# A hybrid decoder layer on one core: engine orders fixed by a table, wider value products, the solve's row spread in two fp32r passes

## The chip, the core and the metric

The kernel runs on one core of a Trainium2 chip. Five engines work from queues of their own, each strictly in the order of its queue: TensorE (PE, with its weight loads PEld), VectorE (DVE), ScalarE (ACT), GpSimd (POOL) and SyncE (SP), which issues most DMAs here. They meet at semaphores. The metric is the device time of one execution in microseconds, the median of several runs; lower is better.

## The reference

One decoder layer over 512 tokens of width 1024, batch 1, all in float32. Two mixers share an input projection: sparse attention with 8 heads in 2 groups, and a gated DeltaNet with 4 heads of width 128 in chunks of 64. Cut to what matters:

```python
def reference(x, w_in, ...):
    h = x @ w_in[l]
    y_a = nsa_attention(nsa_q, cmp_k, cmp_v, slc_k, slc_v, win_k, win_v, nsa_gate, ...) @ w_nsa_out[l]
    y_b = gated_deltanet(gdn_qkv, gdn_beta, gdn_decay, gdn_gate, ...) @ w_gdn_out[l]
    mix = (sigmoid(gate_a) * y_a + sigmoid(gate_b) * y_b) @ w_o[l]
    x = layer_norm(DEEPNORM_ALPHA * x + mix, ln1_g[l], ln1_b[l])
    f = conv_ffn(x, ffn_w_up[l], ffn_conv_w[l], ffn_w_down[l])
    return layer_norm(DEEPNORM_ALPHA * x + f, ln2_g[l], ln2_b[l])

def nsa_attention(...):
    o = g[0] * o_cmp + g[1] * o_slc + g[2] * o_win     # three softmax branches, each probabilities @ values

def gated_deltanet(...):
    qkv = silu(causal_dwconv(qkv, conv_w))             # four taps per channel
    m = where(strict, einsum('bhncd,bhnsd->bhncs', kb, k) * decay, 0.0)
    T = lax.linalg.triangular_solve(eye + m, eye, left_side=True, lower=True, unit_diagonal=True)
    # u = T @ (v*beta), w = T @ (kb*exp(gcum)), then a scan over the chunks
```

With 8 blocks of 64 keys and the best 8 chosen, the selected branch sees all causal keys, as the window branch of 512 does.

## The kernel before

**Precision.** Most products are made of three fp32r products: each operand is split into a rounded part (wh, xh, mh) and a remainder (wl, xl, ml), and `product` adds rounded x rounded, rounded x remainder and remainder x rounded in PSUM (L262, L264, L265). ACT rounds a weight block (L248; or DVE or POOL, L250), DVE or POOL forms its remainder (L252). Small products of the mixers run in plain fp32.

**Stages.** `token_major` projects what is needed with tokens on the partitions (PSUM tiles pb) while x arrives. Then come 40 projections of 128 columns each (`gemm_t`, PSUM tile gps in two banks, 24 products of 512 columns for one). They are the work with which PE fills the time of the two mixers. After the mixers come the output projections (pm), the projection w_o with the first normalisation (pw), the FFN's up-projection (pu, 22 steps of two), and its down-projection (px, py, pz) by a scheme with sums of weight blocks, which POOL forms by eight adding DMAs (`sums`, wsum).

**DeltaNet, for each of the 4 heads.** `gdn_k`, `gdn_q` and `gdn_v` make a projection, a convolution of four taps and SiLU: the first tap goes from PSUM into acc on ACT (L405), three more follow on DVE (L413) or, by a table, as an ACT product and a POOL sum (L410, L411). The projection's PSUM bank is free again when the last tap has read it. `gdn_mid` makes decays and the matrix m from products of k with k and q (L507). `gdn_tri` starts the triangular solve with blocks of 16 rows: lo is the masked m, f16 its sums folded to 16 columns, gx spreads f16 over rows with the mask "row", and a product with the block mask "same" sums over partitions (L529; first 512, then 256 columns). Fifteen dependent pairs of small DVE instructions (tmp L536, xs L537) invert the blocks, and z (L539) puts them back on the diagonal. `gdn_inv` joins blocks of 16 to 32, 64 and 128 (transposes of z, products of z with m and ym with x), `gdn_out` runs over the four pieces of 128 tokens, `gdn_gate` ends it.

**Attention, for each of the 8 heads.** Units of query blocks t (128 tokens) and branches: `scores` makes scores (L806, L807), exponentials and the scaling; `flip` transposes the probabilities sc (L839) into slots of pth (rounded) and ptl (remainder) and multiplies by the values vcat into pout (L856). The order of units was (branch 0, t 2), (0, 3), (1, 2), (1, 3), (both, 0), (both, 1). Of a product, 256 columns are two query blocks, t 0 and 1 or t 2 and 3, for one key block; a zeroed slot stands where key block 3 meets t 2.

**What sets the order.** ORDER is a list of steps (q queries, k keys, p and c compression, a and b the halves of a head's attention, i j v m n w o y the DeltaNet steps named above, g a merge gate), each recorded with a priority; SHIFT moves a step's priority, ENGINE says which of DVE, ACT and POOL does a given instruction. A scheduler puts the instructions in order by these priorities and by its own view of when each is ready.

Of the kernel before, what the change touches and what calls it, by code (L numbers as in the profile page):

```python
# [130 lines left out]
BUFS = {"w2": 2, 'in': 3, 'st': 6, 'mid': 3, 'out': 5, 'att': 3, 'ob': 1, 'qf': 2, 'kq': 2, 'lx': 1, 'pg': 2, 'pd': 2, 'pa': 3, 'raw': 3, 'wh': 3, 'wl': 3, 'q2': 4, 'mg': 6, 'mr': 3}


@with_exitstack
def body(ctx: ExitStack, tc: tile.TileContext, d, out):
# [205 lines left out]
    upper_r = nsa.tile([128, 128], F32R, name="upper_r")  # L341
    gcw = tiny[:, 0:48].rearrange("p (i h j) -> p i h j", i=3, h=4)
# [171 lines left out]
    def gdn_tri(h):  # L514
# [5 lines left out]
        f16 = sp.tile([128, TT, 16], F32, name="f16", bufs=2)  # L520
        V.tensor_reduce(f16, lo.rearrange("p c (b j) -> p c j b", b=8), axis=AX.X, op=OP.add)
        lx = slot("lx", "lx", (128, TT, 16, 16))
        for r0, n in ((8, 16), (0, 8)):
            rs = slice(r0, r0 + 8)
            sh = (128, TT, 8, n)
            gx = slot("mid", "gx", sh)
            E(f"gx{n}", h).tensor_tensor(gx, bc(f16[:, :, None, :n], sh), bc(C["row"][:, None, rs, None], sh), op=OP.mult)
            pl = dps(sh)
            PE.matmul(pl, C["same"], gx, start=True, stop=True)  # L529
            A.activation(lx[:, :, rs, :n], pl, AF.Copy)  # L530
# [258 lines left out]
    for t in (pth, ptl):  # L789
        G.memset(t[:, :, 6, :].bitcast(F32), 0.0)  # L790
# [35 lines left out]
    def flip(h, u, s):  # L826
# [18 lines left out]
        if t % 2 == 0:  # L845
            return
# [10 lines left out]
        if u < 5:  # L857
            return
# [407 lines left out]
```

## Time and profile before

| what | us |
|---|---|
| median of 3 runs | 851.35 |
| lowest and highest of them | 846.26, 852.24 |
| the profiled execution | 847.99 |
| its span, first to last instruction | 846.2 |
| PE busy in the span | 826.3 |

The profile is of one execution. The span is what all its views divide. "Busy" of PE runs from a product's start to the end of its drain, so that short pauses between products do not show as idle; the chain of work that ended last gives instead the piece of time for which each instruction held the end back. A group's row has line, engine, operation, out<-in, shapes and count, then busy us and mean ns of one, then idle before and who ended it. A row of the waits says which instruction waited for which: us in total, how often, the longest. In rows of instructions in time, the first two columns are the start and the length; x4 means four records together, and a product in plain fp32 leaves two records. In windows each row is a stretch, with the busy time of each engine, its instructions in brackets, the granted share of PE's clock, and the DMA's share and GB/s.

### The profile page before, as it was taken

The page shows a single profiled execution, that of the slowest core. Times are in us where ns is not written, and L with a number is a line of the kernel's source. Part 1 is how long each engine was busy: PE and PEld are TensorE (multiplying, and loading weights), DVE is VectorE, ACT ScalarE, POOL GpSimd, SP SyncE. Part 2 cuts the span into 40 slices and gives each one's busy share as a digit, 9 for nine tenths or more (in the row PEclk, how much of TensorE's full clock was granted, in tenths as well). Part 3 has the DMA queues.
Part 4 walks back from the last instruction along what each step waited for, and adds up shares of the span by engine and source line. Part 5 has one row for each costly group of instructions (what it writes and reads, how often), then busy time and mean ns, then how long its engine had stood idle before and what let it go on. Part 6 is the DMA issues. An engine that isn't in the chain of part 4 may idle for free.

```text
span 846.2 us, 11884 instructions
## 1 busy us (share of the span) xinstructions
PE 826.3 (98%) x4226; PEld 681.4 (81%) x4226; DVE 597.3 (71%) x1276; ACT 403.0 (48%) x890; POOL 164.3 (19%) x160
## 2 busy tenths in 40 slices
PE   9899899999999999999999999999999999999996
PEld 8777688777778778888888898888888888887874
DVE  5855579986867866674457637777777777768786
ACT  4464377575456777532234113444444444556531
POOL 0354442233136111102200003111112111100000
PEclk9999899999999999999999999999999999999998
DMA  7223111002101110254346007998975922575662
GB/s 273 95 83 100 54 48 51 26 26 75 45 32 66 35 51 26 88 178 134 125 137 237 25 2 269 266 244 253 205 223 153 225 88 77 161 247 176 198 213 100
DMA packets 35051, 108.05 MB, mean 128 GB/s; under 512 B 3248, under 2 KB 4400, under 8 KB 34608
## 3 DMA queue, kind: packets, MB, share of 16 engines
q1 hardware_dynamic: 27696, 84.23, 30.6%
q0 software_dynamic: 7296, 23.07, 11.5%
q8 instruction: 33, 0.54, 0.3%
q14 instruction: 26, 0.21, 0.1%
HBM read 105.19 MB, written 25.17 MB: 154 GB/s over the span
## 4 chain that ended last, share of the span: by engine, by line
PE 84%; DVE 10%; DMA 2%; issue 2%; ACT 1%; SPq 0%; POOL 0%; DVEq 0%; ACTq 0%; POOLq 0%
PE pu L262 9%; PE pu L264 9%; PE pu L265 9%; PE gps L262 7%; PE gps L264 7%; PE gps L265 7%; PE px L1147 5%; PE pz L1147 3%; PE pout L856 2%; PE aps L839 2%; PE pw L1022 2%; PE pw L1023 2%; PE pw L1021 2%; PE pm L265 2%; PE pm L262 2%; PE pm L264 2%
## 5 line engine op out<-in xcount | busy, mean ns | idle before, releaser
L252 DVE TENSOR_TENSOR wl<-raw,wh 128x512 fp32r<-128x512 f32 x140 | 114.1, 816 | 66.9 <-ACT wh L248 62.5
L248 ACT ACTIVATE wh<-raw 128x512 fp32r<-128x512 f32 x136 | 85.5, 631 | 151.4 <-PE pu L264 103.8
L262 PE MATMUL pu<-mh,wh 128*128 128x512 f32 (+1 forms) x384 | 142.7, 372 | 0.0
L264 PE MATMUL pu<-ml,wh 128*128 128x512 f32 (+1 forms) x384 | 142.6, 371 | 0.0
L265 PE MATMUL pu<-mh,wl 128*128 128x512 f32 (+1 forms) x384 | 142.6, 371 | 0.0
L262 PE MATMUL gps<-xh,wh 128*128 128x512 f32 x320 | 129.3, 405 | 3.6 <-DVE xs L537 2.2
L264 PE MATMUL gps<-xl,wh 128*128 128x512 f32 x320 | 129.1, 404 | 0.0
L265 PE MATMUL gps<-xh,wl 128*128 128x512 f32 x320 | 126.8, 398 | 0.0
L265 PEld LDWEIGHTS pu<-mh,wl 128*128 128x128 f32 x384 | 72.3, 188 | 12.6
L262 PEld LDWEIGHTS pu<-mh,wh 128*128 128x128 f32 x384 | 72.3, 188 | 12.4
L264 PEld LDWEIGHTS pu<-ml,wh 128*128 128x128 f32 x384 | 72.3, 188 | 12.4
L262 PEld LDWEIGHTS gps<-xh,wh 128*128 128x128 f32 x320 | 60.4, 189 | 16.6 <-issue 2.9
L1103 DVE SCALAR_TENSOR_TENSOR fa<-pu,fcw,fa 128x511 f32<-128x511 f32 x88 | 65.7, 746 | 10.7 <-ACT fa L1100 9.2
L265 PEld LDWEIGHTS gps<-xh,wl 128*128 128x128 f32 x320 | 60.6, 189 | 10.8 <-issue 0.2
L264 PEld LDWEIGHTS gps<-xl,wh 128*128 128x128 f32 x320 | 60.6, 189 | 10.2 <-issue 0.2
L1109 POOL TENSOR_TENSOR fth<-fth,fa 128x512 f32<-128x512 f32 x22 | 28.6, 1302 | 201.8 <-DVE fa L1103 201.8
L252 POOL TENSOR_TENSOR wl<-raw,wh 128x512 fp32r<-128x512 f32 x36 | 46.3, 1288 | 83.0 <-ACT wh L248 68.8
L1080 ACT ACTIVATE wh<-raw 128x512 fp32r<-128x512 f32 x67 | 40.5, 627 | 39.8 <-DMA raw<-wsum 11.1
L1081 DVE TENSOR_TENSOR wl<-raw,wh 128x512 fp32r<-128x512 f32 x67 | 43.8, 685 | 19.4 <-ACT wh L1080 19.2
L812 ACT ACTIVATE sc<-sc,mn 128x384 f32<-128x384 f32 (+2 forms) x64 | 35.8, 560 | 12.9 <-DVE mn L810 10.7
L295 POOL TENSOR_TENSOR rs<-rs,minus_half 128x1 f32<-128x1 f32 x8 | 7.6, 945 | 166.5 <-DVE rs L980 166.5
L1100 ACT ACTIVATE fa<-pu,fcw 128x512 f32<-128x512 f32 x44 | 29.6, 672 | 10.2 <-PE pu L265 10.2
(330 smaller groups left out, 1689.5 us busy)
## 6 DMA issues: line engine op xcount, KB each, us to landing
raw<-in_up SPq DMA_DIRECT2D x44, 512.0 KB, 4.8
raw<-in_wT SPq DMA_DIRECT2D x40, 512.0 KB, 3.5
wsum<-in_down POOLq DMA_DIRECT2D x6, 2816.0 KB, 24.5
raw<-wsum SPq DMA_DIRECT2D x20, 512.0 KB, 4.2
raw<-in_down SPq DMA_DIRECT2D x15, 512.0 KB, 4.4
wsum<-wsum POOLq DMA_DIRECT2D x2, 2816.0 KB, 12.3
raw<-in_wm SPq DMA_DIRECT2D x8, 512.0 KB, 3.6
raw<-in_wo SPq DMA_DIRECT2D x8, 512.0 KB, 3.6
```

What stands on the lines that cost most here:

```text
L248: A.activation(wh, r, AF.Copy)
L252: eng.tensor_tensor(wl, r, wh.bitcast(F32), op=OP.subtract)
L262: i = PE.matmul(ps, wh[k], mh_(k), start=(k == 0), stop=False)
L264: PE.matmul(ps, wh[k], ml_(k), start=False, stop=False)
L265: PE.matmul(ps, wl[k], mh_(k), start=False, stop=(k == n - 1))
L812: A.activation(s[:, i, :n], s[:, i, :n], AF.Exp, scale=-1.0, bias=mn[:, 0, i:i + 1], accum_out=mn[:, 1, i:i + 1])
L1080: A.activation(hi, raw[:, i], AF.Copy)
L1081: V.tensor_tensor(lo, raw[:, i], hi.bitcast(F32), op=OP.subtract)
L1100: A.activation(acc, ps, AF.Copy, scale=w[:, 2:3])
L1103: V.scalar_tensor_tensor(acc[:, n:], ps[:, :S - n], w[:, i:i + 1], acc[:, n:], op0=OP.mult, op1=OP.add)
L1109: G.tensor_tensor(th, th, g[1], op=OP.mult)
L1147: m = PE.matmul(ps, a[x][:, j, ts], w[y], start=first and i == 0, stop=last and i == 2, skip_group_check=True)
```

## The change

**The order.** SHIFT, ENGINE and ORDER have new entries. A new table QUEUES lists for each engine its instructions by number, the number being the place at which the kernel's code makes the instruction. After the body, `queues` ties every instruction to the one ahead of it in the table by an edge that sets the order only and waits for nothing at run time. So the scheduler's choice is replaced by the table, instruction by instruction. In all, the runs of numbers cover 3904 products of PE (3960 before).

**The value products.** The units now go (both, 0), (both, 1), (0, 2), (0, 3), (1, 2), (1, 3). pth and ptl have 13 slots per branch in place of 8; key block k and query block t stand at slot 3k + t. The products of a branch come together after its t 3: key block 0 against all four query blocks (512 columns), 1 against three (384), 2 and 3 against two (256; the zeroed slot is 11).

**The row spread.** f16 gets three parts: the sum, its rounded part and the remainder. Two gx tiles in fp32r are made and multiplied by a rounded copy same_r of the mask, adding up in PSUM. [...]

**Room.** The scratch of the DMAs that POOL issues is set to 4096 bytes per partition.

```diff
+QUEUES = {
+    "PE": """0-9 11-12 10 13-48 50 53 56 49 51-52 54 62-63 59 57 60 64 61 55 71 65 58 66 74-76 68 67 77 72 78 69-70 73 79 89 80 83
...
+def queues(tc):
+    made = {k: [] for k in QUEUES}
+    for i in tc.nc.cur_bb.bb.instructions:
+        k = str(i.engine).split(".")[-1]
+        if k in made and type(i).__name__ != "BassTilePoolBoundary":
+            made[k].append(i)
+    for k, runs in QUEUES.items():
+        last = None
+        for run in runs.split():
+            a, _, b = run.partition("-")
+            for n in range(int(a), int(b or a) + 1):
+                i = made[k][n]
+                if last is not None:
+                    tc.add_manual_dep(i, last.name, mybir.DependencyInfo(
+                        mybir.DependencyClass.NoSync, mybir.DependencyReason.SCHED_ONLY), reason="place in its queue")
+                last = i
...
+        G.tensor_copy(same_r, C["same"])
...
-        f16 = sp.tile([128, TT, 16], F32, name="f16", bufs=2)
-        V.tensor_reduce(f16, lo.rearrange("p c (b j) -> p c j b", b=8), axis=AX.X, op=OP.add)
+        f16 = sp.tile([128, 3, TT, 16], F32, name="f16", bufs=2)
+        V.tensor_reduce(f16[:, 2], lo.rearrange("p c (b j) -> p c j b", b=8), axis=AX.X, op=OP.add)
+        V.tensor_copy(f16[:, 0].bitcast(F32R), f16[:, 2])
+        V.tensor_tensor(f16[:, 1], f16[:, 2], f16[:, 0], op=OP.subtract)
...
-            gx = slot("mid", "gx", sh)
-            E(f"gx{n}", h).tensor_tensor(gx, bc(f16[:, :, None, :n], sh), bc(C["row"][:, None, rs, None], sh), op=OP.mult)
             pl = dps(sh)
-            PE.matmul(pl, C["same"], gx, start=True, stop=True)
+            for i, e in enumerate(("gx", "gy")):
+                gx = slot("mid", "gx", sh, F32R)
+                E(f"{e}{n}", h).tensor_tensor(gx, bc(f16[:, i, :, None, :n], sh), bc(C["row"][:, None, rs, None], sh),
+                                              op=OP.mult)
+                PE.matmul(pl, same_r, gx, start=(i == 0), stop=(i == 1))
...
-    UNITS = [((0, 2),), ((0, 3),), ((1, 2),), ((1, 3),), ((0, 0), (1, 0)), ((0, 1), (1, 1))]
+    UNITS = [((0, 0), (1, 0)), ((0, 1), (1, 1)), ((0, 2),), ((0, 3),), ((1, 2),), ((1, 3),)]
...
-        for br, _ in parts:
-            for k in range(4 if t > 1 else 2):
-                o = pout[:, 256:] if t > 1 else pout[:, :256]
-                b = 2 * k if t > 1 else 4 + 2 * k
-                w = vcat[:, k, br, g].rearrange("p a b -> p (a b)")
-                for i, src in enumerate((pth, ptl)):
-                    PE.matmul(o, w, src[:, br, b:b + 2, :], start=(u == 1 and k == 0 and i == 0), stop=False)
-        if u < 5:
+        for k in range(4):
+            c = min(k, 2)
+            w = vcat[:, k, br, g].rearrange("p a b -> p (a b)")
+            for i, src in enumerate((pth, ptl)):
+                PE.matmul(pout[:, 128 * c:], w, src[:, br, 3 * k + c:3 * k + 4, :],
+                          start=(br == 0 and k == 0 and i == 0), stop=False)
+        if br == 0:
             return
...
+        queues(tc)
```

**Where rows moved.** DVE at the end of the first head's solve, before: tmp and xs are the solve's steps (the last number of the shape is what is left of the block), acc the convolution taps of a projection gps.

```order
L536 TENSOR_TENSOR tmp<-lx,xs 128x4x3
L537 TENSOR_TENSOR xs<-xs,tmp 128x4x3
L536 TENSOR_TENSOR tmp<-lx,xs 128x4x2
L413 SCALAR_TENSOR_TENSOR acc<-gps,tiny,acc 128x511
L537 TENSOR_TENSOR xs<-xs,tmp 128x4x2
L413 SCALAR_TENSOR_TENSOR acc<-gps,tiny,acc 128x510
L536 TENSOR_TENSOR tmp<-lx,xs 128x4
L413 SCALAR_TENSOR_TENSOR acc<-gps,tiny,acc 128x509
L537 TENSOR_TENSOR xs<-xs,tmp 128x4
L539 TENSOR_TENSOR z<-xs,cst 128x512
```

The same solve on DVE now, some steps after its start (kq is the end of another projection's SiLU):

```order
L681 TENSOR_TENSOR tmp<-lx,xs 128x4x13
L554 SCALAR_TENSOR_TENSOR acc<-gps,tiny,acc 128x510
L554 SCALAR_TENSOR_TENSOR acc<-gps,tiny,acc 128x509
L682 TENSOR_TENSOR xs<-xs,tmp 128x4x13
L681 TENSOR_TENSOR tmp<-lx,xs 128x4x12
L682 TENSOR_TENSOR xs<-xs,tmp 128x4x12
L564 SCALAR_TENSOR_TENSOR kq<-th,acc 128x4x128
L681 TENSOR_TENSOR tmp<-lx,xs 128x4x11
L554 SCALAR_TENSOR_TENSOR acc<-gps,tiny,acc 128x511
L682 TENSOR_TENSOR xs<-xs,tmp 128x4x11
L681 TENSOR_TENSOR tmp<-lx,xs 128x4x10
L554 SCALAR_TENSOR_TENSOR acc<-gps,tiny,acc 128x510
```

The taps that stood among the last three of the fifteen step pairs stand among the third to the sixth; one more stands just ahead of the solve and one behind its last step, and z of this head is in POOL's queue.

PE at the first head's spread products, before (aps rows belong to the compressed branch):

```order
L265 MATMUL gps<-xh,wl 128x512
L529 MATMUL dps<-gx,cst 128x512
L741 MATMUL aps<-cu,w_692 128x62
L529 MATMUL dps<-gx,cst 128x256
L747 MATMUL aps<-w_692,gv 128x64 x2
L262 MATMUL gps<-xh,wh 128x512
L264 MATMUL gps<-xl,wh 128x512
```

And now, from the eleventh projection product behind the first spread product (of the rounded part, 512 columns) on:

```order
L403 MATMUL gps<-xl,wh 128x512
L886 MATMUL aps<-cu,w_663 128x62
L892 MATMUL aps<-w_663,gv 128x64 x2
L404 MATMUL gps<-xh,wl 128x512
L674 MATMUL dps<-gx,same_r 128x256
L674 MATMUL dps<-gx,same_r 128x512
```

Two products side by side have become four, spread over 17 projection products, and 61 instead of 49 projection products follow before the first transpose of z.

SP near the start, before:

```order
L214 DMA xr_128<-in_xT 128x512
L218 DMA wB_133<-in_wB 128x576
L214 DMA xr_129<-in_xT 128x512
L241 DMA raw<-in_wT 128x1024 x3
L337 DMA tiny<-in_tiny 128x57
L338 DMA cst<-in_consts 128x1444
L339 DMA ident<-in_consts 128x128
```

And now (xr are slices of x, raw the weight blocks, cst the masks, fcw the FFN's taps; ident went earlier still, ahead of the last five slices of x):

```order
L353 DMA xr_128<-in_xT 128x512
L491 DMA fcw<-in_fcw 128x132
L357 DMA wB_133<-in_wB 128x576
L850 DMA pos<-in_pos 128x32
L353 DMA xr_129<-in_xT 128x512
L476 DMA tiny<-in_tiny 128x57
L380 DMA raw<-in_wT 128x1024
L477 DMA cst<-in_consts 128x1444
L380 DMA raw<-in_wT 128x1024 x6
```

The small constants moved ahead of the last slice of x, and the masks ahead of the second weight block.

More of the change, by code (lines that the diff above doesn't have):

```diff
@@ new lines @@
+1405 1330 1230 1293-1294 1406 1408 1407 1409 1295-1296 1410-1413 1231-1232 1297 1422-1423 1298-1299 1414 1300
+1415-1418 1424-1426 1419-1420 1427 1379-1380 1428 1381-1383 1421 1384-1387 1429-1432 1443-1444 1388 1331-1332
+1389-1391 1433 1392 1434-1435 1445-1446 1436-1438 1447 1439-1440 1448 1441 1449 1453-1454 1393 1442 1301 1394 1450
+1333 1395-1398 1455 1458 1451-1452 1456-1457 1459 1399 1302-1303 1400 1304-1306 1460-1463 1401 1472-1473 1334 1464
+1402 1474-1480 1501 1465 1481-1482 1502 1466-1468 1483 1469-1470 1503 1335 1504 1336-1338 1471 1339-1342 1505-1506
@@ new lines @@
+3874-3875 3845-3858 3876-3879 3859 3880-3881 3860-3865 3882 3866-3870 3883-3903""",
+    "DVE": """0 27 104 1-4 6 5 7 9 8 10-11 13 12 14-15 17 16 18-19 58-61 64 28 22 20 65 23 66 62 67 25 21 63 90 115 72 31-35 73
+36-37 24 38-42 30 43 29 44 26 45-50 102 51-52 74 53-54 68-69 83 55-56 70-71 81 84 82 92-93 85-87 94 75 88 80 76 79 95
+151-153 77 91 107 154 109 164 110-111 108 112 89 113 96-100 166 101 103 165 114 167 212 155 116-118 285 119 105 120
+156-157 121-123 158 124 168 125-126 169 127-128 57 129 106 130-133 78 134-136 170 137-138 213 139-145 172 146-147 173
@@ new lines @@
+55 48 42 51 49 62 47 52 92 66 37 67-68 64 69 57 65 46 58 50 87 56 53 59 61 63 88 90 60 80 75 77 76 86 78 84 71 85
+72-73 70 94 81 74 82 93 91 89 95 79 96-97 83 98-130 132 131 133-134 136 135 137 139 138 140 142 141 143 145 144
+146-147 149 148 150 152 151 153-163""",
+    "SP": """0-7 17 8-12 18 13 25 14-15 19 16 20-23 26-31 24 32-78 84-86 79-81 87-90 82 91 83 92-128 130-135 129 136-159 161 163
+165 167-168 160 162 169 164 166 170-178""",
+}
+def queues(tc):
[14 more added lines that the diff above has]
+                last = i
@@ L341, in body @@
     upper_r = nsa.tile([128, 128], F32R, name="upper_r")
+    same_r = nsa.tile([128, 128], F32R, name="same_r")
     gcw = tiny[:, 0:48].rearrange("p (i h j) -> p i h j", i=3, h=4)
@@ L785, in cmp_attn @@
         PC[g] = (hi, lo)
-    pth = nsa.tile([128, 2, 8, 128], F32R, name="pth")
-    ptl = nsa.tile([128, 2, 8, 128], F32R, name="ptl")
+    pth = nsa.tile([128, 2, 13, 128], F32R, name="pth")
+    ptl = nsa.tile([128, 2, 13, 128], F32R, name="ptl")
     for t in (pth, ptl):
-        G.memset(t[:, :, 6, :].bitcast(F32), 0.0)
-    UNITS = [((0, 2),), ((0, 3),), ((1, 2),), ((1, 3),), ((0, 0), (1, 0)), ((0, 1), (1, 1))]
+        G.memset(t[:, :, 11, :].bitcast(F32), 0.0)
+    UNITS = [((0, 0), (1, 0)), ((0, 1), (1, 1)), ((0, 2),), ((0, 3),), ((1, 2),), ((1, 3),)]
     POUT = {}
@@ L839, in flip @@
                 PE.transpose(pt[:, i, k, :], s[:, i, k * 128:(k + 1) * 128], ident)
-        first = t - 2 if t > 1 else 4 + t
-        own = (slice(br, br + len(parts)), slice(first, first + 2 * t + 1, 2))
+        own = (slice(br, br + len(parts)), slice(t, 4 * t + 1, 3))
         th, tl = pth[:, own[0], own[1], :], ptl[:, own[0], own[1], :]
```

108 lines of the change are left out of this document (102 added, 6 removed), and 5 rows, old and new, of the table QUEUES.

## The prediction

> **What bounds the kernel now.** I read the page first: the engine totals, the granted clock in 40 slices, the chain of work that ended last.
>
> ```profile
> PE 826.3 (98%) x4226; PEld 681.4 (81%) x4226; DVE 597.3 (71%) x1276; ACT 403.0 (48%) x890; POOL 164.3 (19%) x160
> PEclk9999899999999999999999999999999999999998
> PE 84%; DVE 10%; DMA 2%; issue 2%; ACT 1%; SPq 0%; POOL 0%; DVEq 0%; ACTq 0%; POOLq 0%
> ```
>
> PE is busy for 826.3 of 846.2 us, so a change pays where it shortens PE's own work or one of PE's few waits. DVE has 10% of the chain: the waits are mostly for it. The windows say where PE is not full (after the length come PE, PEld, DVE, ACT and POOL busy, then the granted clock).
>
> ```profile
> 0.00:350.00 350.00, 339.81 (x1982) 276.63 (x1983) 251.94 (x757) 204.15 (x568) 106.42 (x108) 0.99 0.21 67
> 350.00:846.00 496.00, 486.54 (x2246) 404.79 (x2244) 345.33 (x519) 198.85 (x323) 57.90 (x52) 0.99 0.58 170
> ```
>
> Up to 350 us, the mixers, PE lacks 350 − 339.8 = 10.2 us. From there on the order of PE's products is unchanged but for the interleaving of the first merges; that stage's 9.5 us (the tail of the down projection and the last normalisation) I leave as they are. PE's own waits by name:
>
> ```profile
> PE gps L262 <- DVE xs L537: 2.2, 1, 2.2
> PE gps L327 <- DVE vm L324: 1.4, 1, 1.4
> PE gps L262 <- ACT tap L410: 1.2, 1, 1.2
> PE dps L395 <- issue: 1.1, 1, 1.1
> PE px L1147 <- ACT w L1080: 0.9, 1, 0.9
> PE aps L839 <- DVE xs L537: 0.6, 1, 0.6
> PE pz L1147 <- DVE wl L1081: 0.6, 1, 0.6
> PE dps L427 <- DVE z L558: 0.5, 1, 0.5
> ...
> PE dps L427 <- POOL z L539: 0.5, 1, 0.5
> PE dps L529 <- DVE gx L527: 0.5, 1, 0.5
> ```
>
> Without the start (L327) and the tail (L1147), the six rows for the mixers besides the first make 4.4 us. The largest wait, in order of time (start, length, engine and line):
>
> ```profile
> 88.24 1.32 POOL L252 TENSOR_TENSOR wl<-raw,wh 128x512 fp32r<-128x512 f32 x1 [0.30 <-ACT wh L248]
> ...
> 88.45 1.14 DVE L537 TENSOR_TENSOR xs<-xs,tmp 128x16 f32<-128x16 f32 x1
> ...
> 89.84 0.17 DVE L537 TENSOR_TENSOR xs<-xs,tmp 128x12 f32<-128x12 f32 x1
> ...
> 91.69 0.75 DVE L413 SCALAR_TENSOR_TENSOR acc<-gps,tiny,acc 128x509 f32<-128x509 f32 x1
> ...
> 92.59 0.65 PE L262 MATMUL gps<-xh,wh 128*128 128x512 f32 x1 [2.21 <-DVE xs L537]
> ```
>
> The projection wants its PSUM bank, which is free once DVE has read it in the convolution taps (acc, L413). These stand in DVE's queue behind the steps of the solve, so the wait put down to xs is really for the taps. A solve step of 0.17 us takes 1.14 us where it starts under a POOL product. And the clock falls right behind the wait:
>
> ```profile
> 88.00:92.70 4.70, 2.49 (x12) 1.79 (x10) 4.48 (x13) 0.33 (x2) 1.32 (x1) 1.00 0.36 112
> 92.70:99.50 6.80, 6.74 (x26) 5.86 (x27) 2.08 (x5) 2.73 (x5) 3.18 (x3) 0.50 0.00 1
> ```
>
> 6.8 us at 0.50 cost 3.4 us. The episode is worth 2.2 + 3.4 = 5.6 us.
>
> **The change, part by part.** What a product costs PE is its distance to the next start, not its duration, in which the drain is counted. The chain gives the distances.
>
> ```profile
> 125.68 0.83 PE pout L856 x7
> ...
> 131.95 0.17 PE aps L807
> ...
> 142.23 0.44 PE aps L839 x4
> ...
> 144.28 0.11 PE aps L839
> 144.39 0.24 PE gps L264
> ```
> ```profile
> 730.28 14.29 PE px L1147 x63
> ```
>
> So 256 columns cost 0.83/7 = 0.119 us, 384 columns 0.17 us (the L807 row here is the one of that width), 512 columns 14.29/63 = 0.227 us.
>
> *Value products.* Per head, branch and part (rounded, remainder) six products of 256 columns, 0.711 us, become one of 512, one of 384 and two of 256: 0.227 + 0.17 + 0.237 = 0.637 us. There are 8 x 2 x 2 = 32 such groups: −2.4 us. PE is full beside them, so all of it counts. Ends: 0, if the products wait for later transposes instead (they now start only when all four row blocks of a branch are there), and −4.0, if the 8 groups less also save a change of precision of 0.2 us each (below). I take −2.4; it is plain counting on a full engine.
>
> *Row spread.* One fp32 product of 512 and one of 256 columns now, and the projection behind them:
>
> ```profile
> 215.11 1.53 PE L529 MATMUL dps<-gx,cst 128*128 128x512 f32 x4 [0.47 <-DVE gx L527]
> ...
> 216.29 0.58 PE L262 MATMUL gps<-xh,wh 128*128 128x512 f32 x1
> ```
>
> Start to start 1.18 us; the four fp32r products are 2 x (0.227 + 0.119) = 0.69 us. Four heads: 4 x 0.49 = −2.0 us. Ends: −3.4 us by the 1.53, and 0, if the longer chain ahead of the product takes it back. That chain gains a rounding and a subtraction of 128x64 and a second gx of each width:
>
> ```profile
> L521 DVE TENSOR_REDUCE f<-lo 128x64 f32<-128x512 f32 x4 | 4.2, 1057 | 1.2 <-POOL lo L519 1.1
> ...
> L527 DVE TENSOR_TENSOR gx<-f,cst 128x512 f32<-128x512 f32 x4 | 3.2, 807 | 0.0
> ...
> L537 DVE TENSOR_TENSOR xs<-xs,tmp 128x60 f32<-128x60 f32 x4 | 1.0, 238 | 0.0
> ...
> L527 DVE TENSOR_TENSOR gx<-f,cst 128x256 f32<-128x256 f32 x2 | 0.8, 411 | 0.0
> ```
>
> With 0.24 for each of the first two (nearest row, 60 columns), that is up to 0.48 + 0.81 + 0.41 = 1.7 us a head, 6.8 us of DVE and POOL in a stage where DVE is idle for 350 − 251.9 = 98 us. It lies beside other work of PE where there is enough between the products of k and the first gx product. In the first head that cover shrinks from 42 projection products and 16 others to 7 and the 16 of the compression, each of which leaves two records:
>
> ```profile
> 68.16 2.37 PE aps L721 x16
> ```
>
> 2.37/8 = 0.30 us each, so 7 x 0.227 + 16 x 0.30 = 6.3 us, against a chain of lo and the wide gx on POOL (1.32 each by the wl row above), the reduction 1.06, the rounding 0.24 and half a microsecond for m, 4.4 us. Behind the gx pair on POOL there wait a root of the norms and three weight remainders. The third head, where PE waits for gx today (0.5), has 13 projections and 8 others for 6 and 20, about as much cover, and 0.24 us more to cover. I add 0.5 us; without any cover it would be 6.8.
>
> *Order, the long wait.* In the first head 49 projection products stand between the last spread product and the first transpose of z; now 61, and six small ones more: 12 x 0.227 = 2.7 us more cover against a wait of 2.2 us. The taps are moved up among the solve steps, and z goes from DVE to POOL. For what is now behind them: the solve ends later on DVE by the taps' three times 0.75 us, less than the cover added. I count the episode as gone: −5.6 us (ends 0 and −5.6).
>
> *Order, the other waits.* Of the 4.4 us and the unlisted waits below 0.5 us, some 6 us in all (10.2 of idle less the 2.2, the 1.4 and the start), I take half, −3.0: the places differ by a few products either way (from the last gx product to z, 30 projections and 63 others become 25 and 56 in the second head, 44 and 7 become 45 and 8 in the third). Ends: +3 and −6.
>
> *Order, more changes of precision.* A run of fp32 products that fp32r follows ends 197 times in the new order, 152 in the old. A single transpose between two projections costs 0.11 us (144.28), as much as each of four in a run (0.44/4), so nothing is paid there, and 27 of the 45 are such. Behind the narrow products of the inverse the next one is late:
>
> ```profile
> 102.58 0.36 PE dps L576 x14
> 102.95 0.43 PE gps L262
> ```
>
> 0.43 for 0.227 is 0.2 us; those do not grow in number. Ends 0 and 45 x 0.2 = 9.0 us; nearest the transposes, I take +1.0.
>
> *Order of SP.* The identity (128x128 f32, 64 KB), the FFN's taps (128x132, 66 KB) and two small transfers now go ahead of the last slice of x or the first weight block, and the masks (128x1444, 722 KB) ahead of the second block.
>
> ```profile
> 6.91 0.47 SPq L218 DMA_DIRECT2D wB<-in_wB  x1
> ```
> ```profile
> 10.00:20.00 10.00, 10.00 (x68) 9.45 (x69) 6.82 (x15) 4.41 (x10) 0.00 (x0) 1.00 0.93 360
> ```
>
> At 360 GB/s the masks delay the second block by 2.0 us, the small ones x by 0.5, and SP needs up to 0.47 us to issue each of the four, 1.9 us. PE is full there and has the 24 products of the first block, 5.4 us, in front: 0 by that cover, +4.4 without; I take +0.5, nearer the full row. The POOL queue loses six weight remainders (wl) and gains taps, gx and scales, 164.3 us being 19% of the span; no term of its own. The smaller DMA scratch touches only the eight sums that POOL issues in the FFN.
>
> **The sum**: −2.4 − 2.0 + 0.5 − 5.6 − 3.0 + 1.0 + 0.5 = −11.0 us. Beside its span of 846.2 the profiled execution took 847.99 us, 3.4 below the median of 851.35; the sum gives 837.0 for it and 840.3 for the median, which I predict.
>
> [...]
>
> **The rivals.** *All waits of the mixers go*: 3.0 more than in the sum, 837.3, and down to 831 if the changes of precision are free too and short waits within "busy" go along. For it: the table is fine enough to place single products. Against: the cover ahead of gx shrinks in the first head and is the same in the third. 0.19. *The waits only move*: 4.4 of arithmetic less 2.0 of costs, 849.0. For it: DVE's queue is served strictly in order, so an early tap delays a solve step that somebody else awaits. 0.24. *The half clock stays* though the wait goes, since something else causes it: −7.6, 843.8; for it the length of 6.8 us, three times the wait, against it that the drop follows the wait directly. 0.10. *Slower*: the first head's episode arises in more heads. A solve step goes from 0.17 to 1.14 us under a POOL product; POOL now also makes the second gx and z. If three more heads wait about 2.2 us and lose the clock too, 3 x 5.6 − 2.4 = +14.4, 865.8; with two, 860.2, so it decides from two such waits of 2 us on. Against it: 98 us of idle DVE, and taps that no longer stand behind the whole solve. 0.11. [...] *The scratch delays the sums*:
>
> ```profile
> wsum<-in_down POOLq DMA_DIRECT2D x6, 2816.0 KB, 24.5
> ```
>
> they land within 24.5 us, and one or two are issued in every two or three of the 22 FFN steps; only if several stood still would the down projection wait, by one landing: some 865. 0.02.
>
> **How the numbers follow.** The forecast has 0.34, with 836 to 846 of its own. A measurement of this kernel tells about 1% from no change: below 842.8 is faster, above 859.9 slower. Faster: 0.31 of the forecast and 0.19, 0.50. Slower 0.11 (the 0.02 for the scratch goes half to each side of the bound, and rounds off). The rest, 0.39, is the same. The range 831 to 853 reaches from the end of "all waits go" past "only move" and leaves out the slower case and some of the fringes.
>
> **What would show it.** Value rows of 512 and 384 columns with a summed distance lower by 2.4 us; L674 without an fp32 row; no PE wait over 1 us behind the first solve, and PEclk 9 in the fifth slice; PE idle before 350 us at 4 to 6 us. It is wrong if a second slice before 350 us shows the clock at 8, if PE waits for DVE's gx or z more than 0.6 us in several heads, or if PE's busy time falls by less than 4 us.

## The result and the profile after

| | before | after |
|---|---|---|
| median, us | 848.81 (4 runs) | 836.94 (4 runs, 834.16 to 838.45) |
| ratio, 95% interval | | 0.9857 [0.9817, 0.9897] |
| the profiled execution, us | 847.99 | 838.45 |
| its span, us | 846.2 | 836.7 |

The change makes the kernel faster by 1.4% of its time; the prediction said 840.3 us in a range of 831 to 853. Before's median has one run more than the 851.35 us of the prediction, so it differs a little. Three executions of the experiments below, one each of after_again, spread_free and yol_wo, took 1.2 to 3.4 times as long as the others of their kernel and are left out of the ratios; that of yol_wo, with PE's clock at 0.75, is the one that was profiled, so its trace is not read here.

The page of the kernel after, the same three lines as before: totals by engine, the granted clock, the chain.

```profile
PE 815.3 (97%) x4162; PEld 675.0 (81%) x4162; DVE 597.7 (71%) x1295; ACT 399.8 (48%) x890; POOL 169.3 (20%) x168
PEclk9999999999999999999999999999999999999998
PE 76%; DVE 12%; DMA 6%; ACT 2%; issue 2%; SPq 1%; DVEq 0%; ACTq 0%
```

PE is busy 11.0 us less and still for 97% of the span. The 8 in the fifth clock slice is gone. But PE's share of the chain fell from 84% to 76%, and DMA has 6% of it where it had 2%: the last cause of a wait now lies more often elsewhere. The windows, as before:

```profile
0.00:350.00 350.00, 339.62 (x1970) 280.08 (x1971) 261.43 (x793) 209.40 (x580) 100.72 (x108) 1.00 0.23 71
350.00:836.00 486.00, 475.68 (x2194) 394.93 (x2192) 336.30 (x503) 190.45 (x310) 68.57 (x60) 1.00 0.57 171
```

PE lacks 350 − 339.6 = 10.4 us up to 350 us, as much as before (10.2). A fixed window is treacherous here, though, because the work in it has moved: the output projection now begins inside it. By the starts of PE's products, stage by stage:

| first product of | before | after | after minus before |
|---|---|---|---|
| output projection (pm) | 355.10 | 338.54 | −16.6 |
| w_o projection (pw) | 442.13 | 431.30 | −10.8 |
| up projection (pu) | 488.60 | 478.46 | −10.1 |
| down projection (px) | 730.12 | 719.98 | −10.1 |
| end of PE's last product | 838.04 | 828.56 | −9.5 |

Merge gates and the output projection are interleaved, in another pattern than before, so pm's row says little and pw's is the first like-for-like line. All of the gain, 10.8 us, is made ahead of it; 1.3 us of it are given back behind it. PE's waits of the kernel after, the largest by name:

```profile
PE pm L403 <- DVE yol L1077: 2.4, 1, 2.4
PE gps L466 <- DVE vm L463: 1.4, 1, 1.4
PE dps L536 <- issue: 1.2, 1, 1.2
PE aps L984 <- DVE xs L682: 0.8, 1, 0.8
PE aps L984 <- DVE sc L968: 0.8, 2, 0.5
PE aps L984 <- ACT sc L966: 0.8, 2, 0.5
PE px L1290 <- DVE rs L1123: 0.7, 1, 0.7
PE aps L568 <- DVE cs L922: 0.7, 1, 0.7
```

The 2.2 us for the projection in the first solve are gone. A wait of the same length, for yol, stands at a new place, the start of the output projection. PE's only wait for gx is now one of 0.14 us (0.5 before).

### The profile page after: what moved, and what is told of

Its sections match the earlier page's. It is cut to its first block, busy times and chain, and to the rows that moved or that the text cites. A ratio compares the mean times of both kernels' runs of the same rounds, so it can differ in the third digit from the quotient of the medians.

```text
span 836.7 us, 11718 instructions
## 1 busy us (share of the span) xinstructions
PE 815.3 (97%) x4162; PEld 675.0 (81%) x4162; DVE 597.7 (71%) x1295; ACT 399.8 (48%) x890; POOL 169.3 (20%) x168
## 4 chain that ended last, share of the span: by engine, by line
PE 76%; DVE 12%; DMA 6%; ACT 2%; issue 2%; SPq 1%; DVEq 0%; ACTq 0%
PE pu L403 10%; PE pu L404 10%; PE pu L401 10%; PE gps L401 8%; PE gps L404 8%; PE gps L403 8%; DVE wl L1224 2%; PE px L1290 2%; DMA raw<-wsum 2%; PE pout L998 2%; PE aps L984 2%; DMA raw<-in_down 1%; PE dps L568 1%; PE pm L404 1%; PE pm L401 1%
## 5 line engine op out<-in xcount | busy, mean ns | idle before, releaser
L391 DVE TENSOR_TENSOR wl<-raw,wh 128x512 fp32r<-128x512 f32 x146 | 118.0, 809 | 58.2 <-ACT wh L387 55.3
L387 ACT ACTIVATE wh<-raw 128x512 fp32r<-128x512 f32 x126 | 79.3, 630 | 131.1 <-PE pu L403 102.0
L403 PE MATMUL gps<-xl,wh 128*128 128x512 f32 x320 | 126.9, 401 | 0.0
L1223 ACT ACTIVATE wh<-raw 128x512 fp32r<-128x512 f32 x67 | 40.2, 626 | 41.6 <-DMA raw<-wsum 15.8
L1224 DVE TENSOR_TENSOR wl<-raw,wh 128x512 fp32r<-128x512 f32 x67 | 43.5, 684 | 20.5 <-ACT wh L1223 20.5
L391 POOL TENSOR_TENSOR wl<-raw,wh 128x512 fp32r<-128x512 f32 x30 | 39.2, 1307 | 19.4 <-ACT wh L387 9.9
L984 PE MATMUL aps<-ident,sc 128*128 128x128 f32 x160 | 33.8, 278 | 2.8 <-DVE xs L682 0.8
## 6 DMA issues: line engine op xcount, KB each, us to landing
wsum<-in_down POOLq DMA_DIRECT2D x6, 2816.0 KB, 23.7
```

Source lines behind the costliest of these rows:

```text
L387: A.activation(wh, r, AF.Copy)
L391: eng.tensor_tensor(wl, r, wh.bitcast(F32), op=OP.subtract)
L403: PE.matmul(ps, wh[k], ml_(k), start=False, stop=False)
L984: PE.transpose(pt[:, i, k, :], s[:, i, k * 128:(k + 1) * 128], ident)
L1223: A.activation(hi, raw[:, i], AF.Copy)
L1224: V.tensor_tensor(lo, raw[:, i], hi.bitcast(F32), op=OP.subtract)
```

## The experiments

Each ratio is to runs of the kernel before on the same chip, made side by side. The experiments stand in three groups, each with its own runs of before: first after_again, table_old, new_free and arith_free, then taps_late, yol, gdec and yol_gdec, then the rest. Two ratios of different groups compare less well than two of one. The kernel after itself came out at 0.987 [0.9847, 0.9893] when it was run again.

| label | what it is | ratio, 95% interval | PE busy, us |
|---|---|---|---|
| after_again | the kernel after | 0.9870 [0.9847, 0.9893] | 815.0 |
| table_old | table, old arithmetic | 0.9929 [0.9914, 0.9943] | 818.9 |
| table_fp32 | table, old row spread | 0.9877 [0.9852, 0.9902] | 816.5 |
| new_free | after without the table | 1.0080 [1.0064, 1.0096] | 824.7 |
| arith_free | before with both pieces of arithmetic | 1.0300 [1.0270, 1.0330] | 833.1 |
| val_free | before with the value products | 1.0351 [1.0319, 1.0383] | 837.0 |
| spread_free | before with the row spread | 1.0363 [1.0316, 1.0409] | 833.1 |
| taps_late | after, taps behind the solve | 0.9935 [0.9914, 0.9957] | 819.2 |
| yol | after, yol ahead of wol | 0.9861 [0.9837, 0.9886] | 818.0 |
| gdec | after, decays ahead of a tap | 0.9885 [0.9858, 0.9911] | 817.1 |
| yol_gdec | both of these | 0.9874 [0.9852, 0.9896] | 817.2 |
| yol_wo | yol, and the first w_o block early | 0.9799 [0.9768, 0.9830] | not read |

**Order and arithmetic apart.** In table_old the table stays; each wide value product is followed at once by its second half, and the row spread is one fp32 product of each width.

```diff
+                if k == 0:
+                    PE.matmul(pout[:, :256], w, src[:, br, 0:2, :], start=first, stop=False)
+                elif k == 1:
+                    PE.matmul(pout[:, 128:384], w, src[:, br, 4:12:7, :], start=False, stop=False)
...
+            PE.matmul(pl, C["same"], gx, start=True, stop=True)
```

> The changed kernel with the same table, but both pieces of arithmetic undone: value products of 256 columns again (each wide one is followed at once by its second half; the units stay in the new sequence), the row spread as one fp32 product of each width, without the rounding, the remainder and the second gx. Theory, arithmetic and order add up and PE is full beside both: 4.8 us more than the changed kernel, 0.9915 of before (841 to 843 us), PE busy 4 to 6 us more. Rival, the longer chain ahead of gx costs what the fp32r products save: only the 2.4 us of the value products come back, 0.989. Rival, order alone is worthless or worse: 1.00.

Measured 0.9929: 0.0059 more than the kernel after in the same group, 5.0 us of 849. The order alone is worth the other 6.0 us (1 − 0.9929, interval 4.8 to 7.3). Both are clear of zero, and the arithmetic's 5.0 us (2.7 to 7.3 by the two intervals) are near the 4.8 that had been counted.

table_fp32 undoes the row spread alone.

> The changed kernel with the same table, the row spread alone undone (one fp32 product of each width; no rounding, remainder and second gx). Theory, its four fp32r products of 0.69 us for 1.3 us of fp32 are its whole price, as the longer chain is covered: 2.0 to 2.4 us more than the changed kernel, about half of what both pieces cost together in this order (table_old), 0.9895 of before, PE busy 1.5 to 2.5 us more. Rival, the chain ahead of gx holds PE: without it PE waits less, same time as the changed kernel, 0.987. Rival, the value products' widths give nothing: all of table_old's 5 us come back, 0.993.

Measured 0.9877, within the intervals of the kernel after; PE is busy 1.2 to 1.5 us more. The spread is worth 0.6 to 1.7 us by the two ratios of the kernel after, less than the 2.0 to 2.4 expected, though the intervals exclude neither that nor zero. From here to table_old it is the value products alone: 0.0052, 4.4 us, between two groups, with intervals that reach from 1 to 8 us.

Without the table the same arithmetic looks different. new_free drops one line:

```diff
-        queues(tc)
```

> The changed kernel without the edges of the table: the new ORDER, SHIFT and ENGINE, the scheduler chooses the order. Theory, the table takes away waits that the scheduler leaves: between arithmetic alone and the whole change, 0.988 to 0.996 of before (839 to 845 us), PE idle before 350 us longer than the 10.4 us of the changed kernel. Rival, the table only writes down what the scheduler would choose with these priorities: 0.986, the same waits. Rival, the priorities serve only the table's search: slower than arithmetic alone, 1.00 or more.

Measured 1.008, slower than before: the number of the last case, though not its comparison, as the arithmetic alone came out slower still (next run). With these priorities the scheduler does not find the table's order, and the table is worth 0.021, 18 us, beside it.

arith_free puts both pieces into the kernel before and lets the scheduler order them.

> The kernel before with the two pieces of arithmetic alone (wide value products, row spread in fp32r, the smaller DMA scratch), the order left to the scheduler with the old ORDER, SHIFT and ENGINE (the entries for the units renamed to follow them). Theory, arithmetic counts in full wherever it stands: 4.8 us of products less (value products 2.4, row spread 2.4 by the distances), PE busy lower by 4 to 6 us, time 0.994 of before (843 to 846 us). Rival, it pays only in an order made for it: waits of PE eat it, time 0.998 or more. Rival, the arithmetic is the whole change and the order nothing: 0.988 or less.

Measured 1.03. The rival that it pays only in its own order, and by far more than that rival said: 4.8 us less arithmetic, 25 us more time (and 2.2% more than the same arithmetic with the new priorities). Which of the two pieces does it was asked next (the diffs are the two parts of the change).

> The kernel before with the value products alone (and the smaller scratch), ordered by the scheduler. Both pieces together took 3% more than before in that order. Theory, it is this piece: the products of a branch stand together behind its last row block and the units come in another sequence, to which the old priorities were not fitted: 1.02 to 1.035 of before, long PE waits for scores, exponentials and z. Rival, it is the row spread's longer chain: 0.995 to 1.00 here. Rival, any edit upsets the scheduler's order alike: 1.01 to 1.02 here and there.

> The kernel before with the row spread alone (and the smaller scratch), ordered by the scheduler. Theory, the longer chain has cover and the order hardly moves: 0.995 to 1.005 of before. Rival, its chain on DVE (the second gx in DVE's queue in every head, as the old table of engines has no entry for it) holds PE at the gx products and z: 1.01 to 1.03. Rival, any edit upsets the scheduler's order alike: 1.01 to 1.02 here and in the run with the value products alone.

Each alone takes 3.5%, and both together take no more. That is nearest to the last case, in which any edit upsets the scheduler's order alike, but by more than its 1.01 to 1.02; for the value products 1.035 is also the end of the theory's range. The largest waits of spread_free:

```profile
PE gps L262 <- ACT qf L696: 6.4, 2, 6.1
PE gps L262 <- DVE mn L820: 3.2, 1, 3.2
PE dps L429 <- DVE z L545: 3.0, 2, 2.6
PE gps L262 <- DVE xs L543: 2.3, 1, 2.3
```

and of val_free:

```profile
PE gps L262 <- ACT qf L690: 6.5, 2, 6.3
PE aps L839 <- ACT sc L821: 2.5, 2, 2.1
PE gps L262 <- DVE xs L537: 2.2, 1, 2.2
```

In both PE stands 6 us at one and the same step (3.9 us in arith_free), a projection waiting for the attention's queries (qf) to leave PSUM, which neither piece touches. In the three runs PE is idle for 40 to 44 us of the span where it was 19.9, and the half clock lasts 17.1, 30.7 and 17.1 us (arith_free, val_free, spread_free; the end of the span left out) where it was 6.8; about half of that time is lost, as from one projection product to the next it was 0.43 us in a window at half clock (40.08 us in the kernel after) and 0.23 at full. In the programs as they are built, PE's list of some 3590 rows differs from that before in 650 to 820 lines in each of the three (a row that moves gives two); the smaller DMA scratch by itself moves none on PE and one or two on DVE and ACT. The likely reading is that the old SHIFT and ORDER fit one program, and that the scheduler's choices fall out otherwise for another. That any edit would do the same is not shown, since no edit that leaves both pieces alone was tried; nor was it explained why the size comes out alike for both.

**The long wait of the first head.** taps_late takes the kernel after and moves two taps and a SiLU product in DVE's queue (168 to 170 in the table) from the middle of the solve to behind its last step; PE's queue stays.

```diff
-158 124 168 125-126 169 127-128 57 129 106 130-133 78 134-136 170 137-138 213 139-145 172
+158 124-128 57 129 106 130-133 78 134-138 213 139-145 168-170 172
```

> The changed kernel, with two convolution taps and the SiLU product behind them moved in DVE's queue from among the middle steps of the first head's solve to behind its last step, as they stood before the change; PE's queue stays. Theory, the place of the taps made the long wait of the kernel before: their PSUM bank comes free some 6 us later, PE waits 2 to 4 us in a projection at about 90 us, and with over 2 us of idle PE in one window of 3.41 us the clock is halved for one or two windows: 4 to 7 us more than the changed kernel, 842 to 845 us, 0.991 to 0.995 of before. Rival, the 12 more projection products ahead of the transposes of z cover it whatever the place of the taps: less than 1 us more, 0.987.

Measured 0.9935, 0.0065 or 5.5 us more than the kernel after. In order of time on PE:

```profile
87.39 0.78 PE L907 MATMUL aps<-kcb,qf 128*128 128x64 f32 x6
92.08 0.80 PE L401 MATMUL gps<-xh,wh 128*128 128x512 f32 x1 [3.91 <-ACT tap L551]
```

and on DVE, the solve's last step and the late taps:

```profile
89.63 0.17 DVE L682 TENSOR_TENSOR xs<-xs,tmp 128x4 f32<-128x4 f32 x1
89.72 1.53 DVE L554 SCALAR_TENSOR_TENSOR acc<-gps,tiny,acc 128x511 f32<-128x511 f32 x2
```

PE waits 3.9 us for the bank that the taps hold (the last of them, on ACT, comes behind the two on DVE), and the clock is halved behind it, as the windows show (PE busy is the first number behind the length, the granted clock the third from the end):

```profile
88.11:91.52 3.41, 0.06 (x1) 0.00 (x0) 2.86 (x12) 0.18 (x1) 0.00 (x0) 1.00 0.00 0
91.52:94.94 3.42, 2.87 (x7) 2.31 (x8) 0.87 (x1) 1.65 (x3) 2.84 (x3) 0.50 0.00 0
```

The wait and half of that window, 3.9 + 1.7 us, are the 5.5. Three instructions in another place bring back an episode of this kind; the 12 more projection products do not cover it. The taps stand further back here than in the kernel before, where they were among the last three step pairs, so the wait is longer than its 2.2 us.

**The new wait for yol.** On DVE in the kernel after, at the output projection:

```profile
344.00 0.69 DVE L1077 TENSOR_TENSOR yol<-yT,yoh 128x512 fp32r<-128x512 f32 x1 [2.55 <-ACT yoh L1075]
346.14 1.23 DVE L1097 TENSOR_TENSOR wol<-raw,woh 128x1024 fp32r<-128x1024 f32 x1 [1.45 <-ACT woh L1096]
347.28 0.69 DVE L391 TENSOR_TENSOR wl<-raw,wh 128x512 fp32r<-128x512 f32 x1
347.88 0.69 DVE L1077 TENSOR_TENSOR yol<-yT,yoh 128x512 fp32r<-128x512 f32 x1
```

The last yol, wanted at 346, stands behind the remainder of a w_o block (wol) that waits 1.45 us for ACT and that nobody needs for another 85 us. yol moves it ahead:

```diff
-711-713 723 714 735 729 715 724 730 725 736 728 726-727 731
+711-713 723 714 729 715 735 724 730 725 736 728 726-727 731
```

> The changed kernel, with one move in DVE's queue: the last remainder of the mixers' output (yol) and the weight remainder beside it (wl) go ahead of the remainder of the w_o block (wol), which waits for its ACT rounding. Theory, PE's longest wait now (2.4 and 2.5 us at 346 us, ahead of the output projection) is made by that order of three DVE instructions alone and nothing stands right behind it: PE no longer waits there, 2.4 us less, and where the wait had halved the clock in a window (as in the repeated run) another 1.7 us: 833 to 835 us, 0.982 to 0.984 of before. Rival, the wait moves on: PE waits the same time a few products later, for wol, a weight remainder or the merge: 837, 0.986.

Measured 0.9861, no change from the kernel after: the rival. The wait for yol is gone, and the largest by name is another:

```profile
PE pm L401 <- ACT wh L387: 2.3, 2, 2.1
```

The chain of yol at this place (start, length, and who held the end back):

```profile
344.34 0.96 ACT woh L1096
...
345.32 1.23 DVE wol L1097
...
346.57 3.83 DMA raw<-in_wm
...
350.49 0.63 ACT wh L387
```

The next weight block can only be loaded once wol has read a buffer for raw weights, and its 3.8 us of DMA follow. There are three such buffers, and one is taken by the first w_o block, loaded from 331 us on and used by ACT only at 351. yol_wo therefore also moves that block's rounding and remainder (467 on ACT, 728 on DVE) ahead of the third yol:

```diff
-456 465 468 458 469 471-472 467 466 475
+456 465 467-468 458 469 471-472 466 475
...
-711-713 723 714 735 729 715 724 730 725 736 728 726-727 731
+711-713 723 728 714 729 715 735 724 730 725 736 726-727 731
```

> The changed kernel with the yol move, and with the first w_o block's rounding (ACT) and remainder (DVE) moved ahead of the third yol: in the trace this block lies in one of the three buffers for raw weights from 331 to 352 us, and the next weight block of the output projection waits 6 us for a buffer; its landing is what PE waited for once yol was out of the way. Theory, with the buffer free at about 343 us the block lands at about 347 us, 4 us before PE wants it: no wait over 0.6 us in the first 25 us of the output projection, 2.5 us less, 4 with the half clock behind it: 833 to 836 us, 0.981 to 0.984 of before, faster than the changed kernel. Rival, 2.3 us more of ACT and DVE ahead of the third yol make PE wait there instead: 0.986 or more.

Measured 0.9799 [0.9768, 0.9830], five executions from 831.15 to 836.61 us: faster than before by 2.0%, and below the kernel after in either of its measurements (0.9857 and 0.9870), though those belong to other groups, and its interval overlaps with that of the first. That the wait went as the theory has it is not shown, for want of a trace that can be compared.

**The wait ahead of the decays.** gdec moves one tap on DVE behind the last two steps of the decays:

```diff
-26 45-50 102 51-52 74 53-54 68-69
+26 45-50 102 51-54 74 68-69
```

> The changed kernel, with one move in DVE's queue: the convolution tap that waits for ACT goes behind the two last steps of the decays (sacc, gdec). Theory, PE's wait of 1.2 us ahead of the decay products (36 us, put down to issue) is this tap standing in front of them: the wait falls below 0.4 us, 1 us less in time (0.985 to 0.986, too little to tell by the clock alone), the decay products start 1 us earlier after the last projection product. Rival, the decays wait for something else (ACT's exponential, the constants): the wait stays at 1.2 us.

Measured 0.9885: no gain. In the trace of gdec on DVE, POOL and PE:

```profile
35.76 1.27 POOL L391 TENSOR_TENSOR wl<-raw,wh 128x512 fp32r<-128x512 f32 x1
35.77 1.29 DVE L530 SCALAR_TENSOR_TENSOR gdec<-sacc,ea 128x16 f32<-128x16 f32 x1
...
37.09 0.75 DVE L554 SCALAR_TENSOR_TENSOR acc<-gps,tiny,acc 128x511 f32<-128x511 f32 x1
37.16 0.81 PE L536 MATMUL dps<-gdec,cst 128*128 128x16 f32 x6 [1.00 <-PE gps L404]
...
39.23 0.56 PE L401 MATMUL gps<-xh,wh 128*128 128x512 f32 x1 [1.26 <-ACT tap L551]
```

The step gdec now meets a POOL remainder and takes 1.29 us where it took 0.20, so the decay products still wait 1.0 us; and the tap, later by as much, holds a PSUM bank for which PE waits 1.3 us more. So the tap is no longer what the decays wait for, as the theory had it, but the wait hardly shrank (1.2 to 1.0 us), and another came up behind it.

> Both moves together, four DVE instructions in all. Theory, PE is the bound behind both places and the gains add up: 3.4 to 5 us less than the changed kernel, 832 to 834 us, 0.980 to 0.982 of before. Rival, one of the gaps reopens later, 835 or more.

Measured 0.9874, as the kernel after; both gaps had reopened, as above.

**The half clock.**

> The changed kernel once more, as the base for the others on the same chip: 0.986 of the kernel before (about 837 us), within 0.4%. Where the half clock falls is a question of its own. If the 1.4 us wait ahead of the decays (36 us) is by itself enough to halve the clock, the stretch of half clock behind it comes again; if it needed a certain place of that wait on a fixed grid of 3.41 us (all changes of clock in the two traces lie a whole multiple of 3.413 us behind the first one: 25 and 27 times before, 10 and 11 times after), it may be missing, or stand elsewhere, again a whole multiple of 3.413 us behind the start of full clock.

Measured: the time again; the half clock of 40 us is missing, and one stands at 347 us. How this goes is told in the last section.

## Why the prediction was right, point by point

It came out at 836.94 for 840.3, the ratio at 0.9857 for a predicted 840.3/851.35 = 0.987. The mechanism of the largest term, the long wait, held, and the arithmetic came near its count. That the sum fits so well is partly luck: the other waits grew where they were to shrink, and many short delays that the sum did not price went, which made up for it. By its terms, up to the first pw product:

*Value products, −2.4.* In agreement with the runs, as far as they can tell, but the sign that I named for it fails. The summed distance of these rows is 25.7 us before and 26.4 after. The reason is where they stand. In the chain of the kernel after:

```profile
170.90 0.24 PE aps L952
171.14 0.23 PE pout L998
171.38 0.17 PE dps L721 x2
...
171.81 0.36 PE dps L721 x14
172.17 0.61 PE pout L998 x2
```

Behind an fp32r product (L952) one of 512 columns takes 0.23 us, as predicted. Behind fp32 products the 512 and the 384 columns take 0.61 where 0.23 + 0.17 = 0.40 was counted. Over all of them the medians are 0.118, 0.175 and 0.235 us behind fp32r, and 0.202, 0.259 and 0.329 behind fp32: 0.08 to 0.09 more at each width. The last fp32 record ahead of such a product shows 0.028 in place of 0.109 us, 0.081 less. So by these figures nothing is lost; the end of the fp32 product is booked on its follower. Before, 12 of 192 value products stood behind fp32, now 41 of 128: 29 × 0.084 = 2.4 us of other work in these rows, and single waits of up to 0.7 us besides. On the chip, with the table kept, the widths are worth 4.4 us with an interval that holds 2.4.

*Row spread, −2.0, and its chain, +0.5.* The rows of L529 sum to 4.85 us of distances, those of L674 to 3.42: −1.4, and somewhat more with the ends booked on followers. The chain cost PE nothing that a wait would show: its only wait for gx is 0.14 us, 0.5 before. −1.5 together were predicted; undoing it cost 0.6 to 1.7 us, which is not clear of zero.

*The long wait, −5.6.* The mechanism was right, and taps_late shows it. Of the size, the wait went in full (2.4 us by distances). The half clock did not all go: it cost 3.4 us before (6.8 us at 0.50) and 1.7 after (3.4 us at 0.50), at another place, 40 us. Net −4.1. The prediction took the half clock for part of this one wait; in these traces it also follows others, and such a one was there (1.2 us ahead of the decays).

*The other waits, −3.0.* Mis-sized in both directions. PE's idle gaps over 0.25 us ahead of the first pw product come to 9.2 us before and 10.1 after, the first head's 2.2 among those that went: so the others grew by 3.1, and 2.4 of that is the wait for yol, which I could have found by reading DVE's new queue at the mixers' end as I read it in the first solve. Of the gain of 10.8 us, with 5.0 for the arithmetic (table_old), 1.7 for the clock and −0.9 for these gaps, 5.0 remain. By difference they are many delays below 0.25 us, which a view of idle time does not show because PE's drains cover them (a projection product is busy for 0.39 us, and the next starts 0.23 us behind it). The starts of the products bear this out: what each distance has beyond the median of the same product, where that is below 0.25 us, sums to 15.9 us ahead of pw before and 7.9 after, 1.7 of the difference being the clock. In table_old, the old arithmetic in the new order, it is 7.7, so these delays go with the order; which moves took them away is open. "PE idle at 4 to 6 us" was thus the wrong sign to look for (10.4), and "no PE wait over 1 us behind the first solve" failed with the wait for yol, while "PE busy falls by 4 us or more" held (11.0).

*Changes of precision, +1.0.* Nearer zero: what a follower has more, 0.084, its predecessor has less.

*Order of SP, +0.5.* The last token-major product ends at 25.80 for 25.51, the first decay product starts at 37.97 for 37.38; in the repeated run at 25.33 and 37.54. Within 0.6 us, as predicted.

*From 350 us on, 0.* 1.3 us more in both runs of the kernel after, in pw (0.7, and 0.3 in the repeated run) and in the down projection; the pages of the profile name no single cause, and none was sought.

*The rivals.* "All waits of the mixers go" did not come: the idle time is the same. "The waits only move" was wrong for the change as a whole, but right for the moves made in it to gain time, all but yol_wo. "The half clock stays" came in part, by one window at another place; "the episode in more heads" and "the scratch delays the sums" did not come (six of the eight sums land in 23.7 us by the median, 24.5 before).

## What to carry to other kernels

Price the arithmetic and the order apart before believing either: the same 5 us of less work on PE were worth 5 us in an order written out for them, and came with a loss of 25 us in an order that a scheduler chose with priorities fitted to another program. Where every engine's queue is fixed, moving one instruction ahead of another gained nothing here while the next link of the chain behind the wait, a buffer and the DMA that fills it, or the tap and its bank, stayed; the one move that gained took that link along. Read who waits next before you move an instruction. And compare stages by the start of a like-for-like product, and products of one kind only behind the same kind of predecessor.

## What was not expected of the hardware

In the traces of the kernels before and after, every change of the granted clock ahead of PE's last product lies a whole multiple of 3.413 us behind the moment at which it first becomes full: before, 25 and 27 such steps, after, 10 and 11. The windows shown here are cut at these steps, the grid. Those of the kernel before at the long wait (PE busy is the first number behind the length, the granted clock the third from the end):

```profile
89.30:92.71 3.41, 1.20 (x6) 0.72 (x4) 3.27 (x11) 0.18 (x1) 0.26 (x1) 1.00 0.50 154
92.71:96.12 3.41, 3.35 (x14) 2.86 (x15) 1.25 (x3) 2.72 (x5) 2.32 (x3) 0.50 0.00 0
```

The kernel after, at the decays and at the wait for yol:

```profile
36.66:40.08 3.42, 2.19 (x13) 1.85 (x13) 1.96 (x5) 2.44 (x4) 3.42 (x5) 1.00 0.00 0
40.08:43.49 3.41, 3.41 (x10) 2.67 (x9) 2.96 (x6) 1.19 (x2) 1.43 (x3) 0.50 0.50 154
343.86:347.28 3.42, 2.32 (x11) 1.58 (x9) 1.83 (x2) 1.80 (x3) 0.00 (x0) 1.00 0.10 38
347.28:350.69 3.41, 2.07 (x9) 1.73 (x10) 3.08 (x6) 0.00 (x0) 0.00 (x0) 1.00 0.48 159
350.69:354.10 3.41, 3.41 (x17) 2.83 (x16) 2.22 (x3) 1.58 (x2) 0.00 (x0) 1.00 0.50 154
```

And the same kernel run again, at the wait for yol:

```profile
343.74:347.15 3.41, 0.94 (x5) 0.56 (x4) 3.14 (x5) 0.24 (x1) 0.00 (x0) 1.00 0.24 54
347.15:350.57 3.42, 3.42 (x10) 2.65 (x9) 1.78 (x3) 1.58 (x2) 0.00 (x0) 0.50 0.71 237
```

One and the same wait of 2.4 to 2.5 us cost no clock where the grid cut it in two (1.1 and 1.35 us idle), and a window at half clock, 1.7 us, where it fell into one (2.47 us idle). In the whole of the traces of before and after, up to PE's last product, one window at full clock had 1.9 us of idle PE or more, the 2.21 at 89.30, and the next was at half clock; of the five between 1.0 and 1.9 us (1.14 and 1.18 before; 1.23, 1.10 and 1.35 after) the next was so after one, the 1.23 at 36.66; of the 475 below 1.0 us after none. In rows of other runs it was so after 3.35 us idle (taps_late, at 88.11), 2.26 (gdec, at 36.06) and 2.01 (yol, at 353.05), and not after the 1.0 at 36.54 in the repeated run.

The window at 36.66 is the exception, and it orders itself if work is counted and not idleness. With 0.443 ns for each column of an fp32r product (0.227 us / 512) and 0.842 ns for each column of an fp32 record (0.431 us / 512, the wide spread product before), it was filled to 0.37, as the decays' six records have 16 columns each, and the window at 89.30 to 0.31; the four without half clock behind them to between 0.50 and 0.63. This is an estimate, worked out from the products' starts in these two traces and tested on no others; what sets the clock is not shown.

A small DVE step under a POOL remainder, 1.14 us in place of 0.17 in the solve, came again where a step was moved under one (gdec, 1.29 for 0.20 us), and undid the move.
